# The last chunk of the down projection by seven products, a bank of its own for one product of the up projection, and another order of VectorE's and ScalarE's work between the two

## The chip, the cores and the metric

The kernel runs on one core of a Trainium2 chip. The time is that of the device for one execution, in microseconds (us); three runs of the kernel before gave 1249.63, 1249.86 and 1253.42, median 1249.86. The trace is that of one profiled execution of it.

## The reference, cut to what matters

One decoder layer on 1024 tokens of width 1024 in fp32: attention, a residual, an MLP with squared ReLU, a residual and a last RMSNorm. The change touches only what follows the attention:

```python
v = rmsnorm(h, mlp_norm_g)
hid = square(relu(v @ w_up))         # (1024 x 1024) @ (1024 x 4096)
h = h + hid @ w_down                 # (1024 x 4096) @ (4096 x 1024)
out = rmsnorm(h, final_norm_g)
```

Every fp32 operand of a matmul is held as a pair: a rounded high part and the difference to it, the low part. One product of such pairs takes three matmuls (high by high, high by low, low by high). The high part is a CAST of ScalarE (ACT), the low part a subtraction of VectorE (DVE) or GpSimd (POOL); `split2` does both.

## The kernel before

**Up.** The 4096 columns of `w_up` are done in 16 "quads" of 256 columns. A quad is a product of 2 by 2 blocks done with seven products in Winograd's form (`quads`, L1226 to L1289, one `step` for each product), each of 12 matmuls with 512 columns. Its banks in PSUM: tag "pa" (3 banks) for products 1 and 2, tag "bcd" (5 banks) for b, c and d. Product 5 goes to bank d, VectorE adds it to u2 and gets u4 (L1251); product 3 then goes on accumulating in the same bank d, and VectorE reads it once more (L1261, with u2). ScalarE copies product 1 out of "pa" (L1237, `p1`). The quads' results and their sums S1 to S4, the seven left operands of the down projection, go to DRAM (`store_hid`, `hv_dram`), queued on SyncE (SP) by `flush`. The weights of a quad are loaded and prepared one quad ahead (`weights`, `quad_w`: two loads from `w_up`, ten splits by CAST and GpSimd, four sums on VectorE, L1203 to L1206). The last two quads, 14 and 15, are done side by side, product by product; they store their four plain blocks only, to `hl_dram`, for the last chunk.

**The seam.** While quads 14 and 15 run, `w_down`'s first chunk is loaded and prepared: VectorE splits it and forms four differences of its blocks (L1373, L1376, L1379, L1382, tile `wr`), among the reads of the quads' banks. The down projection takes all eight banks of PSUM over (`dn_ps`), so its first tiles wait until VectorE has read the last bank of up.

**Down.** The 4096 rows of `w_down` are eight chunks of 512. Chunks 0 to 6 are done by `down(c)` (L1349 to L1401), with seven products in the order 1, 2, 3, 5, 7, 6, 4. A product has four tiles of 128 rows; a tile is six matmuls into a bank of its own, which VectorE adds into the accumulator of that product (`acc[i]`, L1401). For each product GpSimd makes the low part of the left operand (`ar`, L1076), VectorE or GpSimd that of the right one, and VectorE forms four differences a chunk.

**The last chunk** is done plainly, 192 matmuls (L1448 to L1455). Ahead of it the seven accumulators are folded into the four blocks of h by seven additions for each of four rows of tiles (L1423 to L1429; L1427 and L1428 on GpSimd). The first eight tiles use eight banks and go over the four parts of the contraction together; the other eight are done one by one, six or more matmuls after each other. VectorE adds each tile to its block (L1458), ScalarE squares it and sums (L1437), GpSimd makes the factor of the RMSNorm (L1439, L82, L83), VectorE multiplies (L1442, two instructions for 128 rows of the output) and SyncE stores.

Which instruction stands where on VectorE, ScalarE and GpSimd is decided by a scheduler from the program order; TensorE's order is written out by hand. Each engine then runs its own queue in order.

Of the kernel before, what the change touches and what calls it, by code (L numbers as in the profile page):

```python
# [23 lines left out]
def tile_hymba_block(  # L24
# [1316 lines left out]

    def load_acc():
# [3 lines left out]
        for q in range(4):  # L1346
            nc.gpsimd.tensor_sub(acc[4][:, q], acc[4][:, q], acc[7][:, q])

    def down(c):  # L1349
# [35 lines left out]
        for i in DORD:  # L1385
# [3 lines left out]
            prep(i)  # L1389
            for q in range(4):  # L1390
                ps = dn_ps.tile([P, 512], F32, name="dn", tag="dn")
                n = 0
                for u in range(2):
                    for a, b in ((0, 0), (0, 1), (1, 0)):
                        nc.tensor.matmul(ps[:], av[:, a, u, q * P:(q + 1) * P], bv[i][:, b, u], start=(n == 0), stop=(n == 5))  # L1395
                        n += 1
# [6 lines left out]
    for c in range(NQ // 2 - 2):  # L1403
        down(c)
    hr = [load_ar(hl_dram[:, u]) for u in range(2)]
    for u in range(2):
        split2(lh[u][:, 0], lh[u][:, 1], hr[u][:], nc.gpsimd)
    down(NQ // 2 - 2)


    lw = load_wr(NQ // 2 - 1)
    hr += [load_ar(hl_dram[:, u]) for u in range(2, 4)]
    lhr = dnr_pool.tile([P, 2, 2, T], F32R, name="lhr", tag="wr")
    lh += [lhr[:, 0], lhr[:, 1]]
    lb = []
    for u in range(4):
        lb.append(s8([P, 2, D]))
        split2(lb[u][:, 0], lb[u][:, 1], lw[:, u], nc.vector)
        if u >= 2:
            split2(lh[u][:, 0], lh[u][:, 1], hr[u][:], nc.gpsimd)  # L1420
    for q in range(4):
        g = {i: acc[i][:, q] for i in acc}
        nc.vector.tensor_add(g[2], g[2], g[1])  # L1423
        nc.vector.tensor_add(g[6], g[6], g[1])
        nc.vector.tensor_add(g[5], g[5], g[6])
        nc.vector.tensor_add(g[3], g[3], g[5])
        nc.gpsimd.tensor_add(g[4], g[4], g[6])  # L1427
        nc.gpsimd.tensor_add(g[4], g[4], g[7])  # L1428
        nc.vector.tensor_add(g[7], g[7], g[5])  # L1429
    fin = {}  # L1430

    def finish_half(t, dh, hx):
        if dh == 0:
# [4 lines left out]
        if dh == 1:
            nc.gpsimd.tensor_add(ss[:, 2:3], ss[:, 0:1], ss[:, 1:2])  # L1439
            rsqrt_mean(ss[:, 3:4], ss[:, 2:3], D, 1, nc.gpsimd)  # L1440
            for sl, hv in zip(halves, hs):
                nc.vector.scalar_tensor_tensor(y[:, sl], hv, ss[:, 3:4], gfb[:, sl], ALU.mult, ALU.mult)  # L1442
                if t == NT - 1:
                    nc.sync.dma_start(out[t * P:(t + 1) * P, sl], y[:, sl])
            if t < NT - 1:
                nc.sync.dma_start(out[t * P:(t + 1) * P, :], y[:])
# [59 lines left out]
```

## Time and profile before

| | us |
|---|---|
| median of three runs | 1249.86 |
| the profiled execution | 1253.01 |
| its span, first to last instruction | 1251.1 |
| TensorE busy | 1164.1 (93%) |
| VectorE busy | 954.6 (76%) |
| GpSimd busy | 640.7 (51%) |
| ScalarE busy | 531.6 (42%) |

Times in the rows below are microseconds from the start of the span, so 1251.1 is the end; the chunks 1 to 6 of down lie between about 950 and 1196, the last chunk from 1196.6 to 1242. "Busy" counts an engine's instructions without overlap. A wait such as "PE pd L1082 <- DVE u L1251" is idle time of TensorE ahead of the matmul of line 1082 into tile `pd`, ended by VectorE's instruction of line 1251.

### The profile page before, as it was taken

The numbers are of one execution on the slowest core, as the hardware profiler recorded it, in microseconds if no ns is written. First come the engines' busy times: TensorE is split into PE (matmuls) and PEld (weight loads), VectorE is DVE, ScalarE is ACT, GpSimd is POOL, SyncE is SP. The second block draws the span as 40 slices with busy tenths as digits, with TensorE's granted clock in tenths as the row PEclk, the third lists the DMA queues.
The fourth block names the chain that finished last, engine by engine and source line by source line (L and its number), as shares of the span: only waits on it lengthen the run. The fifth ranks groups of instructions, "written<-read, shape, count | busy, mean of one in ns | idle before, by whom it ended". The sixth has DMA issues, their size and how long they took to land. (4 is left out here: it accounts for less than half of the span.)

```text
span 1251.1 us, 15875 instructions
## 1 busy us (share of the span) xinstructions
PE 1164.1 (93%) x5448; PEld 946.6 (76%) x5448; DVE 954.6 (76%) x1302; ACT 531.6 (42%) x1078; POOL 640.7 (51%) x537
## 2 busy tenths in 40 slices
PE   9998988888799999999599999999889999999997
PEld 8887766666678888887477788777668888888875
DVE  8686499999997873564878965656386899888995
ACT  6434456666766761345422222222225333334402
POOL 3433544545643361315645654545448666668652
PEclk9999999999999999999799999999989999999999
DMA  6425734342712233674336534343658434446103
GB/s 216 130 60 183 179 80 97 77 112 48 225 46 86 68 136 135 204 249 136 130 126 206 177 122 156 123 155 129 223 193 304 153 108 167 155 166 200 53 1 135
DMA packets 100288, 176.70 MB, mean 141 GB/s; under 512 B 9072, under 2 KB 53616, under 8 KB 99440
## 3 DMA queue, kind: packets, MB, share of 16 engines
q1 hardware_dynamic: 100208, 175.70, 43.8%
q8 instruction: 43, 0.70, 0.2%
q14 instruction: 37, 0.30, 0.1%
HBM read 110.13 MB, written 52.95 MB: 130 GB/s over the span
## 5 line engine op out<-in xcount | busy, mean ns | idle before, releaser
L1395 PE MATMUL dn<-s,s 128*128 128x512 f32 x1176 | 269.9, 392 | 4.6 <-DVE ho L1278 4.3
L1395 PEld LDWEIGHTS dn<-s,s 128*128 128x128 f32 x1176 | 222.2, 189 | 52.2 <-DVE ho L1278 4.7
L1076 POOL TENSOR_TENSOR s<-s,s 128x512 fp32r<-128x512 f32 x84 | 121.4, 1462 | 113.1 <-ACT s L1075 112.9
L1076 POOL TENSOR_TENSOR s<-ar,s 128x1024 fp32r<-128x1024 f32 x49 | 131.8, 2694 | 65.2 <-ACT s L1075 65.2
L1401 DVE TENSOR_TENSOR acc<-acc,dn 128x512 f32<-128x512 f32 x184 | 117.9, 677 | 31.4 <-PE dn L1395 31.3
L1075 ACT CAST s<-s 128x512 fp32r<-128x512 f32 x84 | 49.6, 619 | 177.9 <-DMA s<-in_w_up_dram 71.0
L1075 ACT CAST s<-wr 128x1024 fp32r<-128x1024 f32 x53 | 55.6, 1052 | 146.6 <-PE dn L1395 61.0
L1082 PE MATMUL pa<-b,s 128*128 128x512 f32 x384 | 97.2, 407 | 11.8 <-ACT p L1237 4.5
L1082 PEld LDWEIGHTS pa<-b,s 128*128 128x128 f32 x384 | 74.2, 196 | 30.8 <-ACT p L1237 5.7
L542 POOL TENSOR_TENSOR b<-b,w 128x512 f32<-128x512 f32 (+2 forms) x57 | 58.0, 1018 | 60.8 <-DVE w L536 41.4
L488 PE MATMUL mm<-xh,wt 128*128 128x512 f32 x256 | 87.8, 395 | 0.0
L549 PE MATMUL tr<-zid,b 128*128 128x128 f32 x288 | 52.6, 290 | 35.1 <-DVE al L557 25.1
L549 PEld LDWEIGHTS tr<-zid,b 128*128 128x128 f32 x288 | 33.5, 143 | 57.9 <-DVE al L557 43.1
L1076 DVE TENSOR_TENSOR s<-wr,s 128x1024 fp32r<-128x1024 f32 x32 | 64.8, 2024 | 6.1 <-ACT s L1075 5.6
L1076 POOL TENSOR_TENSOR s<-wr,s 128x1024 fp32r<-128x1024 f32 x21 | 51.5, 2453 | 29.4 <-ACT s L1075 29.4
L536 DVE TENSOR_TENSOR_SCAN w<-w,zid 128x129 f32<-128x129 f32 (+1 forms) x64 | 64.7, 1014 | 1.0 <-ACT w L531 0.8
L263 PE MATMUL acc<-wt,xh 128*128 128x448 f32 (+1 forms) x256 | 62.7, 379 | 1.3 <-ACT xh L214 1.3
L1082 PE MATMUL pd<-b,s 128*128 128x512 f32 x192 | 49.5, 409 | 8.3 <-DVE u L1251 4.2
L1075 ACT CAST s<-ar 128x1024 fp32r<-128x1024 f32 x49 | 51.3, 1047 | 12.5 <-DMA ar<-hv_dram 10.7
L1082 PE MATMUL pb<-t,s 128*128 128x512 f32 x192 | 49.2, 406 | 6.8 <-ACT s L1075 6.7
L488 PEld LDWEIGHTS mm<-xh,wt 128*128 128x128 f32 x256 | 48.5, 190 | 8.3 <-issue 0.2
L263 PEld LDWEIGHTS acc<-wt,xh 128*128 128x128 f32 x256 | 47.7, 188 | 9.0 <-ACT xh L214 2.0
(349 smaller groups left out, 2800.9 us busy)
## 6 DMA issues: line engine op xcount, KB each, us to landing
ar<-hv_dram SPq DMA_DIRECT2D x49, 512.0 KB, 3.7
s<-in_w_up_dram SPq DMA_DIRECT2D x32, 512.0 KB, 4.8
wr<-in_w_down_dram SPq DMA_DIRECT2D x16, 1024.0 KB, 7.1
hv_dram<-s SPq DMA_DIRECT2D x56, 256.0 KB, 2.1
hv_dram<-ho SPq DMA_DIRECT2D x42, 256.0 KB, 2.0
wr<-in_w_in_dram SPq DMA_DIRECT2D x24, 256.0 KB, 2.9
raw<-in_w_o_dram SPq DMA_DIRECT2D x8, 512.0 KB, 3.5
ht<-h_dram SPq DMA_DIRECT2D x8, 512.0 KB, 4.2
```

The costliest lines, as they stand in the source:

```text
L263: nc.tensor.matmul(accs[t][:, :width], a[:, kk, t * P:(t + 1) * P], wts[kk][:, b, :width], start=(kk == 0 and p == 0), stop=done)
L488: nc.tensor.matmul(ps[:], wt[:, a, k % 4, :], b[:, k, tsl], start=(n == 0), stop=(n == 3 * ND - 1))
L536: nc.vector.tensor_tensor_scan(rv, rv, inject, init, ALU.mult, ALU.add)
L542: eng.tensor_mul(b[:, :n], b[:, :n], w[:, 1:n + 1])
L549: nc.tensor.transpose(tr[:, j * P:(j + 1) * P], sb_a[h, Q, C, j][:, s * P:(s + 1) * P], identf[:])
L1075: nc.scalar.copy(hi, src)
L1076: eng.tensor_sub(lo, src, f(hi))
L1082: nc.tensor.matmul(ps, w[:, a, k, :], bv[:, b, k, :], start=start and n == 0, stop=n == last, skip_group_check=True)
L1395: nc.tensor.matmul(ps[:], av[:, a, u, q * P:(q + 1) * P], bv[i][:, b, u], start=(n == 0), stop=(n == 5))
L1401: nc.vector.tensor_add(dst, dst, ps[:])
```

## The change

1. *Product 3 of up* gets a bank "e" of its own out of the same five: bank d is read once (u4), and bank e is added to u4 where bank d was added to u2.
2. *Quads 14 and 15* form and store S1 to S4 as the others do: fourteen stores where there were eight, and eight more instructions of VectorE. The second half of quad 15's weights comes after products 1 and 2 in program order. The right operands of products 5, 7, 6 and 4 of chunk 0 are prepared behind the last sum s4 of quad 15.
3. *The last chunk* is `down_last`: seven products in the order 1, 6, 5, 3, 2, 7, 4, of 24 matmuls each. Products 1, 6, 5 and 3 accumulate in the same four banks; VectorE reads each partial sum, after product 1 into acc2, after 6 into acc4, after 5 into acc7, after 3 into acc3. Product 2 has the four other banks; product 7 takes the first four, and product 4 goes on in them. The old folds are done in between, four instructions of 128 by 512 for each, queued behind the last read of their product: on GpSimd 6+=1, 4+=7, 4+=6, on VectorE 5+=6, 3+=5, 2+=1, 7+=5. The four sums of blocks of `w_down` go into a tile `lx`.
4. *The output* has four buffers where it had two; rows t = 0 are multiplied by ScalarE and GpSimd, the others by VectorE in groups of rows.

```diff
     def store_hid(q, v, ap):
         c, u = divmod(q, 2)
-        if c < NQ // 2 - 1:
-            held.append((hv_dram[c][:, v, u], ap))
-        elif v < V_S1 or v == V_A21:
-            f_, th = {V_A11: (0, 0), V_A21: (0, 1), V_A12: (1, 0), V_A22: (1, 1)}[v]
-            held.append((hl_dram[:, 2 * u + f_, th * 512:(th + 1) * 512], ap))
+        held.append((hv_dram[c][:, v, u], ap))
...
-        return w
-
-    ws_, st = {}, {}
-
-    def weights(q):
+        yield
+
+    ws_, st, wgen = {}, {}, {}
+
+    def weights(q, steps=2):
         pre = q < NPRE
-        ws_[q], st[q] = quad_w(q, pre), {}
+        if q not in ws_:
+            ws_[q], st[q] = {}, {}
+            wgen[q] = quad_w(q, pre, ws_[q])
+        for _ in range(steps):
+            next(wgen[q])
...
             elif what == 3:
-                prod(s_["d"][:], w[V_S4], B22, False, True)
+                prod(bank("e"), w[V_S4], B22, True, True)
                 s_["c12"] = o2_tile("ho")
-                nc.vector.tensor_add(s_["c12"][:], s_["d"][:], s_["u2"][:])
+                nc.vector.tensor_add(s_["c12"][:], s_["e"][:], s_["u4"][:])
                 relu2(s_["c12"][:], s_["c12"][:])
-                if q >= NQ - 2:
-                    store_hid(q, V_A21, s_["c12"][:])
-                    return
...
                 store_hid(q, V_A12, c21[:])
-                if q >= NQ - 2:
-                    return
                 s4 = o2_tile("s4")
-                nc.vector.tensor_sub(s4[:], c21[:], s_["s2"][:])
+                s_["end"] = nc.vector.tensor_sub(s4[:], c21[:], s_["s2"][:])
                 store_hid(q, V_S4, s4[:])
...
-    weights(NQ - 1)
+    weights(NQ - 1, 1)
     flush()
     last2 = [NQ - 2, NQ - 1]
     quads(last2, (1, 2))
+    weights(NQ - 1, 1)
...
     gfb = fin_pool.tile([P, D], F32, name="gfb")
-    ys = [fin_pool.tile([P, D], F32, name=f"y{n_}") for n_ in range(2)]
-    fss = [fin_pool.tile([P, 4], F32, name=f"fss{n_}") for n_ in range(2)]
+    ys = [fin_pool.tile([P, D], F32, name=f"y{n_}") for n_ in range(4)]
+    fss = [fin_pool.tile([P, 4], F32, name=f"fss{n_}") for n_ in range(4)]
     dn_pool = ctx.enter_context(tc.tile_pool(name="dn_pool", bufs=1, reuse_waits="tile"))
-    lh = [dn_pool.tile([P, 2, T], F32R, name=f"lh{u}") for u in range(2)]
...
+
+    def dn_mm(ps, av, b_, q, start):
+        n = 0
+        for u in range(2):
+            for a, b in ((0, 0), (0, 1), (1, 0)):
+                nc.tensor.matmul(ps[:], av[:, a, u, q * P:(q + 1) * P], b_[:, b, u], start=start and n == 0, stop=n == 5,
+                                 skip_group_check=True)
+                n += 1
 
     def down(c):
         if c == 0:
@@ -1386,77 +1388,105 @@
             ar = ars[i] if i in ars else load_hv(c, i)
             av = s8([P, 2, 2, 512])
             split2(av[:, 0], av[:, 1], ar[:].rearrange("p (u t) -> p u t", u=2), nc.gpsimd)
-            prep(i)
+            if c == 0 and i not in DORD[:3]:
+                with tc.issue_after(st[NQ - 1]["end"].ins):
+                    prep(i)
+            else:
+                prep(i)
...
+    def finish_half(t, dh, hx):
+        if t not in fin:
+            fin[t] = (fss[t % 4], ys[t % 4], {})
+        ss, y, hs = fin[t]
+        hs[dh] = hx
+        nc.scalar.activation(acc[6][:, t % 4], hx, AF.Square, accum_out=ss[:, dh:dh + 1])
+        if len(hs) == 2:
+            nc.gpsimd.tensor_add(ss[:, 2:3], ss[:, 0:1], ss[:, 1:2])
+            return rsqrt_mean(ss[:, 3:4], ss[:, 2:3], D, 1, nc.gpsimd)
+
+    def finish(t):
+        ss, y, hs = fin[t]
+        for d in range(2):
+            sl = halves[d]
+            if t == 0:
+                nc.scalar.activation(y[:, sl], hs[d], AF.Copy, scale=ss[:, 3:4])
+                nc.gpsimd.tensor_mul(y[:, sl], y[:, sl], gfb[:, sl])
+            else:
+                nc.vector.scalar_tensor_tensor(y[:, sl], hs[d], ss[:, 3:4], gfb[:, sl], ALU.mult, ALU.mult)
+            if t == NT - 1:
+                nc.sync.dma_start(out[t * P:(t + 1) * P, sl], y[:, sl])
+        if t < NT - 1:
+            nc.sync.dma_start(out[t * P:(t + 1) * P, :], y[:])
+
+    def down_last():
+        c = NQ // 2 - 1
+        wr = load_wr(c)
+        lx = dnr_pool.tile([P, 4, D], F32, name="lx", tag="wr")
+        w4 = wr[:].rearrange("p (u a) d -> p a u d", a=2)
+        b11, b12, b21, b22 = [w4[:, a, :, d * 512:(d + 1) * 512] for a in range(2) for d in range(2)]
+        t1, t2, t4, t3 = [lx[:, n_].rearrange("p (u d) -> p u d", u=2) for n_ in range(4)]
+        form = {1: (b11,), 6: (t2, b22, t1), 5: (t1, b12, b11), 3: (b22,), 7: (t3, b22, b12), 2: (b21,), 4: (t4, b21, t2)}
+        g = acc
+        V, G = nc.vector, nc.gpsimd
+        fold = {1: ((G, 6, 1), (G, 4, 7)), 6: ((V, 5, 6), (G, 4, 6)), 5: ((V, 3, 5),), 3: ((V, 2, 1), (V, 7, 5))}
+        for i in (1, 6, 5, 3, 2, 7, 4):
+            ar = load_hv(c, i)
+            av = s8([P, 2, 2, 512])
+            split2(av[:, 0], av[:, 1], ar[:].rearrange("p (u t) -> p u t", u=2), nc.gpsimd)
+            bv = s8([P, 2, 2, 512])
+            if i == 6:
+                nc.vector.tensor_sub(*form[5])
+            if len(form[i]) > 1 and i != 5:
+                nc.vector.tensor_sub(*form[i])
+            split2(bv[:, 0], bv[:, 1], form[i][0], nc.gpsimd if i in (3, 7, 4) else nc.vector)
+            if i in (1, 7, 2):
+                banks = [dn_ps.tile([P, 512], F32, name="dn", tag="dn") for _ in range(4)]
+                if i == 7:
+                    cbanks = banks
+            elif i == 4:
+                banks = cbanks
+            to = {1: 2, 6: 4, 5: 7, 3: 3, 7: 7, 2: 2, 4: 4}[i]
+            for q in range(4):
+                dn_mm(banks[q], av, bv, q, i in (1, 7, 2))
+                read = nc.vector.tensor_add(g[to][:, q], g[to][:, q], banks[q][:])
+                if i == 3:
+                    finish_half(q, 1, g[3][:, q])
+                elif i == 2:
+                    rs3 = finish_half(q, 0, g[2][:, q])
+                elif i == 7:
+                    finish_half(4 + q, 1, g[7][:, q])
+                elif i == 4:
+                    finish_half(4 + q, 0, g[4][:, q])
+            if i == 2:
+                with tc.issue_after(rs3.ins):
+                    finish(0)
+            elif i == 7:
+                with tc.issue_after(read.ins):
+                    for t in range(1, 4):
+                        finish(t)
+            elif i == 4:
+                with tc.issue_after(read.ins):
+                    for t in range(4, NT):
+                        finish(t)
+            with tc.issue_after(read.ins):
+                for eng, a, b in fold.get(i, ()):
+                    for q in range(4):
+                        eng.tensor_add(g[a][:, q], g[a][:, q], g[b][:, q])
...
+    down_last()
```

On VectorE, in the last chunk, before: `acc`n is the accumulator of product n, `dn` a bank of PSUM, `s8` a split operand; the folds begin while chunk 6's products 6 and 4 are still read.

```order
L1424 TENSOR_TENSOR acc6_8731<-acc6_8731,acc1_8726 128x512
L1401 TENSOR_TENSOR acc6_8731<-acc6_8731,dn_10724 128x512
L1076 TENSOR_TENSOR s8_10792<-wr_10773,s8_10792 128x1024
L1401 TENSOR_TENSOR acc4_8732<-acc4_8732,dn_10741 128x512
L1401 TENSOR_TENSOR acc4_8732<-acc4_8732,dn_10749 128x512
L1425 TENSOR_TENSOR acc5_8729<-acc5_8729,acc6_8731 128x512
L1401 TENSOR_TENSOR acc4_8732<-acc4_8732,dn_10757 128x512
L1426 TENSOR_TENSOR acc3_8728<-acc3_8728,acc5_8729 128x512
L1401 TENSOR_TENSOR acc4_8732<-acc4_8732,dn_10765 128x512
L1429 TENSOR_TENSOR acc7_8730<-acc7_8730,acc5_8729 128x512
```

And now, from the last read after product 6 to the first read after product 3:

```order
L1462 TENSOR_TENSOR acc4_8770<-acc4_8770,dn_10820 128x512
L1485 TENSOR_TENSOR acc5_8767<-acc5_8767,acc6_8769 128x512 x4
L1462 TENSOR_TENSOR acc7_8768<-acc7_8768,dn_10817 128x512
L1462 TENSOR_TENSOR acc7_8768<-acc7_8768,dn_10818 128x512
L1462 TENSOR_TENSOR acc7_8768<-acc7_8768,dn_10819 128x512
L1075 TENSOR_TENSOR s8_10996<-wr_10805,s8_10996 128x1024
L1462 TENSOR_TENSOR acc7_8768<-acc7_8768,dn_10820 128x512
L1485 TENSOR_TENSOR acc3_8766<-acc3_8766,acc5_8767 128x512 x4
L1462 TENSOR_TENSOR acc3_8766<-acc3_8766,dn_10817 128x512
```

The same banks dn_10817 to dn_10820 are read after 1, 6, 5 and 3, and four folds stand as one piece between two sets of reads of them; before, each tile had a bank that nothing continued.

On VectorE behind that, before: the last fold, the first reads of the last chunk, the first rows of the output.

```order
L1429 TENSOR_TENSOR acc7_8730<-acc7_8730,acc5_8729 128x512
L1458 TENSOR_TENSOR acc2_8727<-acc2_8727,dn_10825 128x512
L1458 TENSOR_TENSOR acc3_8728<-acc3_8728,dn_10826 128x512
L1458 TENSOR_TENSOR acc2_8727<-acc2_8727,dn_10827 128x512
L1458 TENSOR_TENSOR acc3_8728<-acc3_8728,dn_10828 128x512
L1442 SCALAR_TENSOR_TENSOR y0_8737<-acc2_8727,fss0_8739,gfb_8736 128x512
```

And now, from the last read after product 3 to the first after product 7:

```order
L1462 TENSOR_TENSOR acc3_8766<-acc3_8766,dn_10820 128x512
L1485 TENSOR_TENSOR acc2_8765<-acc2_8765,acc1_8764 128x512 x4
L1485 TENSOR_TENSOR acc7_8768<-acc7_8768,acc5_8767 128x512 x4
L1462 TENSOR_TENSOR acc2_8765<-acc2_8765,dn_10999 128x512
L1462 TENSOR_TENSOR acc2_8765<-acc2_8765,dn_11000 128x512
L1462 TENSOR_TENSOR acc2_8765<-acc2_8765,dn_11001 128x512
L1462 TENSOR_TENSOR acc2_8765<-acc2_8765,dn_11002 128x512
L1462 TENSOR_TENSOR acc7_8768<-acc7_8768,dn_11065 128x512
```

Eight folds and the reads of product 2 now stand ahead of the read of bank 11065, in which product 4 goes on.

On VectorE at the seam, before: `wr` is the chunk of `w_down`, `ho` a block of quad 14 or 15, `pd` and `pc` their banks.

```order
L1255 TENSOR_TENSOR ho_8629<-pc_8616,u4_8599 128x512
L1076 TENSOR_TENSOR s8_8807<-wr_8545,s8_8807 128x1024
L1117 SCALAR_TENSOR_TENSOR ho_8629<-ho_8629 128x512
L1255 TENSOR_TENSOR ho_8645<-pc_8632,u4_8614 128x512
L1376 TENSOR_TENSOR wr_8545<-wr_8545 128x2x512
L1117 SCALAR_TENSOR_TENSOR ho_8645<-ho_8645 128x512
L1261 TENSOR_TENSOR ho_8660<-pd_8586,u2_8569 128x512
L1117 SCALAR_TENSOR_TENSOR ho_8660<-ho_8660 128x512
L1379 TENSOR_TENSOR wr_8545<-wr_8545 128x2x512
L1261 TENSOR_TENSOR ho_8675<-pd_8601,u2_8584 128x512
L1382 TENSOR_TENSOR wr_8545<-wr_8545 128x2x512
L1117 SCALAR_TENSOR_TENSOR ho_8675<-ho_8675 128x512
```

And now, in the same place, with `pe` the new bank:

```order
L1254 TENSOR_TENSOR ho_8659<-pc_8646,u4_8628 128x512
L1112 SCALAR_TENSOR_TENSOR ho_8659<-ho_8659 128x512
L1260 TENSOR_TENSOR ho_8675<-pe_8662,u4_8613 128x512
L1112 SCALAR_TENSOR_TENSOR ho_8675<-ho_8675 128x512
L1263 TENSOR_TENSOR s1_8678<-ho_8675,ho_8643 128x512
L1266 TENSOR_TENSOR s3_8680<-ho_8520,ho_8675 128x512
L1269 TENSOR_TENSOR s2_8682<-s1_8678,ho_8520 128x512
L1260 TENSOR_TENSOR ho_8697<-pe_8684,u4_8628 128x512
L1112 SCALAR_TENSOR_TENSOR ho_8697<-ho_8697 128x512
L1263 TENSOR_TENSOR s1_8700<-ho_8697,ho_8659 128x512
L1266 TENSOR_TENSOR s3_8702<-ho_8535,ho_8697 128x512
L1269 TENSOR_TENSOR s2_8704<-s1_8700,ho_8535 128x512
```

The four differences of `wr` have gone behind the last sum of quad 15, and s1, s3 and s2 of both quads have come in.

On ScalarE where quad 15's weights are made and quad 14's bank is copied (`p1`), before:

```order
L1075 CAST s8_8452<-s8_8449 128x512 x2
L1241 ACTIVATE ho_8408<-pa_8335 128x512
L1075 CAST a22_8457<-s8_8449 128x512
L1075 CAST s8_8464<-s8_8449 128x512
L1237 COPY p1_8494<-pa_8481 128x512
L1075 CAST s8_8464<-s8_8449 128x512
```

And now:

```order
L1074 CAST s8_8466<-s8_8463 128x512 x2
L1240 ACTIVATE ho_8421<-pa_8348 128x512
L1074 CAST a22_8538<-s8_8463 128x512
L1074 CAST s8_8545<-s8_8463 128x512
L1236 COPY p1_8491<-pa_8478 128x512
L1074 CAST s8_8545<-s8_8463 128x512
```

These rows stand as they stood, but for buffer numbers.

## Rows read from the trace of the kernel before

**Rows 1.** Cores: span and mean granted clock.

```profile
core 0: 1251.1 us, clock 0.982
```

**Rows 2.** Windows: length, busy us of each engine (instructions), granted clock, DMA share, GB/s.

```profile
875.00:900.00 25.00, 20.41 (x81) 15.79 (x80) 9.10 (x11) 6.65 (x12) 12.24 (x10) 0.93 0.50 177
...
925.00:950.00 25.00, 21.94 (x86) 17.92 (x87) 13.46 (x18) 8.97 (x12) 11.49 (x6) 0.86 0.94 341
950.00:1158.00 208.00, 208.00 (x918) 171.99 (x917) 178.54 (x189) 81.15 (x84) 148.94 (x59) 1.00 0.50 166
```

**Rows 3.** PE's waits from 715 us to the end: total, times, longest.

```profile
PE pa L1082 <- ACT p L1237: 4.5, 1, 4.5
PE dn L1395 <- DVE ho L1278: 4.3, 1, 4.3
PE pd L1082 <- DVE u L1251: 4.2, 5, 1.5
...
PE dn L1453 <- DVE acc L1401: 0.7, 1, 0.7
PE dn L1395 <- DVE acc L1401: 0.4, 1, 0.4
```

**Rows 4.** SyncE in the loop of `up`: issues of the `w_up` loads.

```profile
830.90 1.51 SPq L1191 DMA_DIRECT2D s<-in_w_up_dram  x2
...
852.17 0.93 SPq L1191 DMA_DIRECT2D s<-in_w_up_dram  x2
...
872.55 0.94 SPq L1191 DMA_DIRECT2D s<-in_w_up_dram  x2
```

**Rows 5.** ScalarE around quad 14's first bank: start, duration, idle before.

```profile
884.49 0.62 ACT L1075 CAST s<-s 128x512 fp32r<-128x512 f32 x1 [4.97 <-DVE s L1203]
885.01 0.58 ACT L1237 COPY p<-pa 128x512 f32<-128x512 f32 x1
```

**Rows 6.** VectorE, the four differences of `w_down` at the seam.

```profile
909.21 3.31 DVE L1373 TENSOR_TENSOR wr<-wr 128x1024 f32<-128x1024 f32 x1
...
919.20 2.80 DVE L1376 TENSOR_TENSOR wr<-wr 128x1024 f32<-128x1024 f32 x1
...
923.85 1.22 DVE L1379 TENSOR_TENSOR wr<-wr 128x1024 f32<-128x1024 f32 x1
...
925.59 1.21 DVE L1382 TENSOR_TENSOR wr<-wr 128x1024 f32<-128x1024 f32 x1
```

**Rows 7.** Groups from 760 us on: busy, mean ns of one, idle before.

```profile
L1076 POOL TENSOR_TENSOR s<-ar,s 128x1024 fp32r<-128x1024 f32 x49 | 131.8, 2694 | 65.2 <-ACT s L1075 65.2
L1401 DVE TENSOR_TENSOR acc<-acc,dn 128x512 f32<-128x512 f32 x184 | 117.9, 677 | 31.4 <-PE dn L1395 31.3
...
L1379 DVE TENSOR_TENSOR wr<-wr 128x1024 f32<-128x1024 f32 x7 | 21.6, 3090 | 5.1 <-POOL s L1076 5.1
...
L1442 DVE SCALAR_TENSOR_TENSOR y<-acc,fss,gfb 128x512 f32<-128x512 f32 x16 | 11.3, 749 | 9.9 <-POOL fss L83 9.9
...
L1423 DVE TENSOR_TENSOR acc<-acc,acc 128x512 f32<-128x512 f32 x4 | 7.0, 1760 | 0.0
...
L1427 POOL TENSOR_TENSOR acc<-acc,acc 128x512 f32<-128x512 f32 x4 | 6.5, 1630 | 11.9 <-DVE acc L1401 7.0 <-DVE acc L1424 4.9
...
L1424 DVE TENSOR_TENSOR acc<-acc,acc 128x512 f32<-128x512 f32 x4 | 2.6, 679 | 0.0
```

**Rows 8.** VectorE's busy time in chunk 6 from one wide instruction to the last.

```profile
1148.30:1170.20 21.90, 21.61 (x20) 1.00 0.56 194
```

**Rows 9.** VectorE, a fold in chunk 6: start, duration.

```profile
1171.34 1.78 DVE L1423 TENSOR_TENSOR acc<-acc,acc 128x512 f32<-128x512 f32 x1
```

**Rows 10.** GpSimd beside it.

```profile
1170.16 2.41 POOL L1076 TENSOR_TENSOR s<-wr,s 128x1024 fp32r<-128x1024 f32 x1 [1.02 <-ACT s L1075]
```

**Rows 11.** TensorE, the last six matmuls.

```profile
1240.41 1.52 PE L1453 MATMUL dn<-s,lhr 128*128 128x512 f32 x6
```

**Rows 12.** VectorE, the last rows of the output.

```profile
1246.77 1.42 DVE L1442 SCALAR_TENSOR_TENSOR y<-acc,fss,gfb 128x512 f32<-128x512 f32 x2 [2.03 <-POOL fss L83]
```

More of the change, by code (lines that the diff above doesn't have):

```diff
@@ L82, in rsqrt_mean @@
         (eng or nc.vector).tensor_scalar(m[:, :width], ssq, 1.0 / n, EPS, ALU.mult, ALU.add)
-        nc.gpsimd.tensor_tensor(dst, m[:, :width], mhalf[:, :width], ALU.pow)
+        return nc.gpsimd.tensor_tensor(dst, m[:, :width], mhalf[:, :width], ALU.pow)
     ctx.enter_context(tc.manual_schedule(engines={mybir.EngineType.PE}))
@@ L1032, in tile_hymba_block @@
     r_dram = [dram.tile([P, HD, HT], F32, name=f"r_dram{n_}") for n_ in range(2)]
-    hv_dram = [dram.tile([P, 7, 2, 512], F32, name=f"hv_dram{c}") for c in range(NQ // 2 - 1)]
-    hl_dram = dram.tile([P, 4, T], F32, name="hl_dram")
-    V_A11, V_A12, V_A22, V_S1, V_S2, V_S3, V_S4, V_A21 = range(8)
+    hv_dram = [dram.tile([P, 7, 2, 512], F32, name=f"hv_dram{c}") for c in range(NQ // 2)]
+    V_A11, V_A12, V_A22, V_S1, V_S2, V_S3, V_S4 = range(7)
     def row_norm(pool, ht, junk, eng=None):
@@ L1186, in o2_tile, with quad_w @@
         return o2_pool.tile([P, 512], F32, name=nm, tag="o2", bufs=11)
-    def quad_w(q, pre):
+    def quad_w(q, pre, w):
         raw = s8([P, ND, 2 * P], F32)
@@ L1193, in quad_w @@
         r11, r12, r21, r22 = [raw[:, HD * d:HD * d + HD, f_ * P:f_ * P + P] for f_ in range(2) for d in range(2)]
-        w = {}
         if not pre:
@@ L1211, in quad_w @@
             w[key] = tl[:, v]
-        return w
-    ws_, st = {}, {}
-    def weights(q):
+        yield
+    ws_, st, wgen = {}, {}, {}
+    def weights(q, steps=2):
         pre = q < NPRE
-        ws_[q], st[q] = quad_w(q, pre), {}
+        if q not in ws_:
[3 more added lines that the diff above has]
+            next(wgen[q])
         if pre:
@@ L1388, in down @@
             split2(av[:, 0], av[:, 1], ar[:].rearrange("p (u t) -> p u t", u=2), nc.gpsimd)
-            prep(i)
+            if c == 0 and i not in DORD[:3]:
[3 more added lines that the diff above has]
+                prep(i)
             for q in range(4):
                 ps = dn_ps.tile([P, 512], F32, name="dn", tag="dn")
[L1392 to L1396, printed above, removed]
+                dn_mm(ps, av, bv[i], q, True)
                 dst = acc[i][:, q]
@@ L1401, in down @@
                     nc.vector.tensor_add(dst, dst, ps[:])
[L1403 to L1429, printed above, removed]
     fin = {}
     def finish_half(t, dh, hx):
-        if dh == 0:
-            fin[t] = (fss[t % 2], ys[t % 2], [])
+        if t not in fin:
+            fin[t] = (fss[t % 4], ys[t % 4], {})
@@ L1435, in finish_half @@
         ss, y, hs = fin[t]
-        hs.append(hx)
-        nc.scalar.activation(y[:, halves[dh]], hx, AF.Square, accum_out=ss[:, dh:dh + 1])
-        if dh == 1:
+        hs[dh] = hx
+        nc.scalar.activation(acc[6][:, t % 4], hx, AF.Square, accum_out=ss[:, dh:dh + 1])
+        if len(hs) == 2:
             nc.gpsimd.tensor_add(ss[:, 2:3], ss[:, 0:1], ss[:, 1:2])
[L1440 to L1446, printed above, removed]
@@ L1448, in tile_hymba_block @@
-    for group in [[(t, dh) for t in range(4) for dh in range(2)]] + [[(t, dh)] for t in range(4, NT) for dh in range(2)]:
-        banks = {k_: dn_ps.tile([P, 512], F32, name="dn", tag="dn") for k_ in group}
-        for u in range(4):
-            for t, dh in group:
-                for n, (a, b) in enumerate(((0, 0), (0, 1), (1, 0))):
-                    nc.tensor.matmul(banks[t, dh][:], lh[u][:, a, t * P:(t + 1) * P], lb[u][:, b, halves[dh]],
-                                     start=(u == 0 and n == 0), stop=(u == 3 and n == 2))
-        for t, dh in group:
-            ps = banks[t, dh]
-            hx = acc[(2, 3, 4, 7)[2 * (t // 4) + dh]][:, t % 4]
-            nc.vector.tensor_add(hx, hx, ps[:])
-            finish_half(t, dh, hx)
+            return rsqrt_mean(ss[:, 3:4], ss[:, 2:3], D, 1, nc.gpsimd)
@@ L1461 @@
+    for c in range(NQ // 2 - 1):
+        down(c)
+    down_last()
 _INS = ["x", "xT", "pos", "gcols", "gfin", "gmlp", "inv_freq", "w_in", "w_q_b", "w_kv_b", "w_o", "w_up", "w_down"]
```

## The prediction

> **What bounds the kernel now.** I read the cores first: one core, span 1251.1 us at a mean clock of 0.982, so the clock is low in a few places only [rows 1]. The windows come next. From 950 to 1158 us, in the chunks of down, TensorE is busy for all of 208.00 us with 918 matmuls: 0.2266 us each, no wait. VectorE is busy for 178.5 of the 208, GpSimd for 148.9 [rows 2]. So down is bound by TensorE, but VectorE has only 14% in hand there. Then TensorE's waits from 715 us on: 4.5 us for ScalarE's copy of product 1, 4.3 us at the seam for a bank, 4.2 us in five waits for u4, and 0.7 and 0.4 us in the last chunks for VectorE's reads [rows 3]. These are what the change can give back, beside the matmuls that it saves. Last the end: TensorE's last matmuls begin at 1240.41 and take 1.52, so they end at 1241.93, and 9.2 us pass until 1251.1 [rows 11].
>
> **Matmuls.** The last chunk goes from 192 to 7 x 24 = 168. 24 x 0.2266 = 5.4 us, on the path, since TensorE is busy there: **-5.4**. A product of 24 takes 5.44 us, a tile of six 1.36.
>
> **Stalls in the new last chunk.** Products 1, 6, 5 and 3 follow each other in the same four banks, and 4 follows 7. Each first tile waits until VectorE has read its bank, and the order shows what VectorE has queued ahead of that read. A read takes 0.64 where reads follow each other (117.9 us for 184), a fold of 512 columns 0.65 alone (2.6 for four), but 1.76 in the group that stands in chunk 6 [rows 7]. The reason is in one pair of rows: GpSimd's instruction of 1170.16 ends at 1172.57, and the fold that began at 1171.34 ends at 1173.12, 0.55 behind it [rows 9, 10]. VectorE's instructions with both inputs in SBUF take turns with GpSimd's; reads of PSUM don't (0.677 over 184 of them, whatever GpSimd does). GpSimd will be busy in the last chunk: seven low parts of `ar` at 2.69, three right operands, twelve folds at 1.63 [rows 7]. Let S be the end of chunk 6 on TensorE.
>
> - A, first tile of product 6, needs the first read after product 1. From the first read of chunk 6's product 7 (S less 16.3, plus 1.36 for the tile: S-15.0) VectorE's queue holds twelve reads and seven wide instructions, then that read. A like stretch of before, with seven wide ones and thirteen reads, took 21.9 us [rows 8]; one read less is 21.3, so the read ends at S-15.0+21.3+0.7 = S+7.0. Needed at S+5.4. Stall 1.6; 0 if the wide ones run alone, up to 9 if each takes 3.09 like the worst group [rows 7].
> - B, first tile of product 3. The last read after product 6 ends 0.7 behind that product; then four folds (F) and the read after product 5 (0.7); product 5 gives 5.44 us of cover. Stall = F + 1.4 - 5.4 = F - 4.0. Alone F is 2.6 and nothing stalls; at 1.76 it is 7.0 and 3.0 us stall; with each fold behind a GpSimd instruction of 2.4 and itself 0.6 behind that, 12 and 8. I take F = 9, since GpSimd has a split or a fold ready nearly all the time in this place: 5.0.
> - C, first tile of product 7, in the same banks, needs product 3's first read: from product 3's start three reads (1.9), a wide low part (2.2, between the 1.21 and 3.31 of [rows 6]), four folds and a read (0.7): 4.8 + F, against 10.9 of cover by products 3 and 2. With F between 7.0 and 9: 0.9 to 2.9. I take 2 (0 to 6).
> - D, first tile of product 4, needs the first read after product 7, behind three reads, eight folds and four reads. Where C has used up the slack, that is 1.9 + F8 + 2.6 + 0.7 against 5.44, so F8 - 0.2. Alone F8 is 5.2: 5.0. With one GpSimd instruction of 2.4 in the way: 7.4. Where C leaves slack, less. I take 5, the middle of the two effects (0 to 14).
>
> Sum 13.6. The 1.1 us of waits for reads that are there now [rows 3] go: **+12.5**.
>
> **A rule beside it.** The Trainium skill, page "SBUF — State Buffer", section "Who interferes with whom", says that a VectorE instruction with two inputs in SBUF contends with a GpSimd instruction that reads SBUF: whichever starts first holds the shared ports for its whole length, and the other is blocked. The rows agree (0.55 us behind GpSimd's end). By the mean of 1.76 B would be 3.0 and the sum 2 us less; by the rule with GpSimd always there first it would be 8, and the sum 3 us more. This rule speaks against four folds in one piece.
>
> **The end.** After the change, counted from product 7's first read, where product 4 starts: three reads 1.9, six multiplications of 0.71 (1.42 for two [rows 12]) 4.3, four reads 2.6, eight multiplications 5.7: 14.5. TensorE ends 5.4 behind that read, so 9.1 remain, and then the store: before, the last multiplication ends at 1246.77 + 1.42 = 1248.19, 2.9 before the end [rows 12]. 12.0 against 9.2: +2.8. If the six also take turns with GpSimd's multiplication of row 0, +2.5 more. I take **+3** (1 to 5). What would hide it is product 4 itself, if the six stood behind its reads; they stand ahead.
>
> **Up.** Product 3 in a bank of its own takes away the five waits for u4, 4.2 us by themselves [rows 3]. I count **0**. The loop runs at the pace of the weights: their loads start every 20.4 to 21.3 us [rows 4], while TensorE's seven products of 12 take 84 x 0.2266 = 19.0, and at the end of the loop the copy that ScalarE owes is itself late: it stands behind the cast that waited 4.97 us for VectorE and begins at 885.01 [rows 5]. ScalarE's order is the same there in the changed kernel. An earlier TensorE so waits longer for that copy. Bounds: -4.2, if the copy too comes earlier, and +1 for more reads in the queue.
>
> **Seam.** VectorE loses four differences there, 3.31 + 2.80 + 1.22 + 1.21 = 8.5 us [rows 6], but gets eight sums, six of them ahead of the first read that down waits for, at 0.7 alone and up to 1.76: 4.2 to 10.6. By itself -4.3 to +2 against the wait of 4.3. Also six stores more of 256 KB go into a window with the DMAs at 0.94 and 341 GB/s [rows 2]: 1.5 MB is 4.6 us there, part of it ahead of the accumulators' loads, which the first adds need. I take **-1** (-5 to +3). The four differences come again behind quad 15's last sum, where products 1, 2 and 3 of chunk 0 hide them (16 us).
>
> **Clock.** The two windows with a wait of over 4 us show a granted clock of 0.93 and 0.86 [rows 2], so mostly the level of 2.4 GHz and for a part that of 1.2, behind a wait. B and D are as long: **+1** (0 to 5).
>
> Sum: -5.4 + 12.5 + 3 + 0 - 1 + 1 = **+10.1**. The profiled execution took 1253.01, its span and 1.9; the median of the runs is 1249.86, 3.1 lower, and the difference should hold for either. Predicted: 1249.9 + 10.1 = **1260.0**. By the bounds of A to D alone (F from 2.6 to 12) the likeliest case reaches from 1253 to 1267.
>
> **Rivals.**
>
> - *The folds run alone.* If GpSimd has done its splits ahead, or its pieces fall beside reads of PSUM, F is 2.6 and A to D give nothing; the waits of 1.1 go too; the end gets +1.5, since product 4 then covers the six multiplications but not its own reads and the eight; the seam -1: -5.4 - 1.1 + 1.5 - 1 = -6.0, **1244**. For it: GpSimd has 28% in hand between 950 and 1158 [rows 2], and folds of 0.679 exist [rows 7]. Against: those 0.679 are of one line, others beside it had 1.76. It decides where four folds take up to 4.0 us. Chance 0.18. This is the other side.
> - *Up and the seam give what their waits say.* If quad 14's copy too is early, 4.2 us come back, and 4.3 at the seam instead of 1: -7.5 on top of the forecast: **1252.5**, little or no change to be seen. Against: the loads' pace and the order on ScalarE. Chance 0.09.
> - *GpSimd becomes the bound.* Ten wide pieces of 2.69 and twelve folds of 1.63 are 46.5 us in 38.1 us of matmuls. Then B is 8 and C 4.8 + 12 - 10.9 = 5.9, D 7.4, A 1.6: 22.9 - 1.1 - 5.4 + 5 - 1 + 1 = +21.4, **1271**. It is also what the rule above would give. For it: the folds of GpSimd wait for reads and then run as pieces of four, beside VectorE's own. Against: the three right operands can be made ahead. Chance 0.13.
>
> **The numbers.** The forecast holds 0.60 of the chance. A difference under 0.3%, 3.7 us, can't be told from none. Faster: the first rival and a tail of the second, 0.19. Same: most of the second that comes below the bound and the lower edge of the forecast, 0.07. Slower: the forecast, the third rival and the second's upper half, 0.74. The range for eight times in ten is 1245 to 1270: it leaves out the lower half of the first rival and the upper half of the third.
>
> **What would show it.** The profile after should show TensorE waiting for VectorE's read of line 1462 three or four times, 1.5 to 5 us each, ahead of products 6, 3, 7 and 4; folds of line 1485 with a mean over 1.4 on VectorE; the waits for u4 gone and the wait for the copy of product 1 longer (about 8 in all, as 4.5 + 4.2 now); from TensorE's end to the span's end 11 to 14 us. Wrong it is if the folds' mean stays under 1.0, if the matmuls of the last chunk run without a wait, or if the wait for the copy of product 1 doesn't grow while those for u4 go.

## The result and the profile after

Five runs of the changed kernel gave 1258.74 to 1262.48 us, median 1261.43; five of the kernel before beside them 1249.63 to 1254.89, median 1253.42. The ratio is 1.0066 with a 95% interval of 1.0041 to 1.0091: slower by 5 to 11 us by that interval, 8.0 by the medians. The profiled execution took 1262.48 us, its span is 1260.7.

TensorE's waits from 715 us to the end (total, times, longest), to be held against [rows 3]:

```profile
PE dn L1347 <- DVE acc L1462: 13.3, 3, 6.2
PE pa L1081 <- ACT p L1236: 7.7, 5, 4.5
PE dn L1347 <- DVE ho L1274: 3.4, 2, 3.0
```

The first row is new: it is the wait for VectorE's reads of the banks that are continued. The waits for u4 are gone, and the one wait of 4.5 for a copy of product 1 has become five of 7.7 in all. Where the 13.3 us lie is shown by TensorE's timeline of the last chunk (start, duration, count, idle before):

```profile
926.58 270.11 PE L1347 MATMUL dn<-s,s 128*128 128x512 f32 x1188 [0.39 <-DVE ho L1274]
1197.68 11.16 PE L1347 MATMUL dn<-s,s 128*128 128x512 f32 x48 [0.99 <-DVE acc L1462]
1215.06 19.24 PE L1347 MATMUL dn<-s,s 128*128 128x512 f32 x72 [6.22 <-DVE acc L1462]
1240.40 7.37 PE L1347 MATMUL dn<-s,s 128*128 128x512 f32 x24 [6.10 <-DVE acc L1462]
```

1164 of the first row's 1188 matmuls bring chunk 6 to its end, at 1191.1 (1196.6 before); the other 24 are product 1 of the last chunk. The waits stand ahead of product 6 (A), of product 3 (B) and of product 4 (D); there is none ahead of product 7 (C). VectorE's timeline says why:

```profile
1204.23 0.69 DVE L1462 TENSOR_TENSOR acc<-acc,dn 128x512 f32<-128x512 f32 x1 [0.56 <-POOL acc L1485]
1204.83 9.49 DVE L1485 TENSOR_TENSOR acc<-acc,acc 128x512 f32<-128x512 f32 x4
1214.24 1.87 DVE L1462 TENSOR_TENSOR acc<-acc,dn 128x512 f32<-128x512 f32 x3
...
1218.29 9.56 DVE L1485 TENSOR_TENSOR acc<-acc,acc 128x512 f32<-128x512 f32 x4
1227.77 2.47 DVE L1462 TENSOR_TENSOR acc<-acc,dn 128x512 f32<-128x512 f32 x4
1230.17 7.10 DVE L1485 TENSOR_TENSOR acc<-acc,acc 128x512 f32<-128x512 f32 x8
1237.19 4.86 DVE L1462 TENSOR_TENSOR acc<-acc,dn 128x512 f32<-128x512 f32 x8
1241.97 6.13 DVE L1426 SCALAR_TENSOR_TENSOR y<-acc,fss,gfb 128x512 f32<-128x512 f32 x6
1248.02 2.47 DVE L1462 TENSOR_TENSOR acc<-acc,dn 128x512 f32<-128x512 f32 x4
```

Four folds take 9.49 us in one piece; the first of the three reads at 1214.24 ends at 1214.9, and TensorE starts at 1215.06. The reads stand behind the folds in VectorE's queue and come behind them. The first row shows one thing more: the read after product 6 goes into acc4 and had to wait for GpSimd's fold 4+=7.

GpSimd's instructions beside the first three of these folds:

```profile
1204.15 2.41 POOL L1075 TENSOR_TENSOR s<-ar,s 128x1024 fp32r<-128x1024 f32 x1
1206.51 2.84 POOL L1075 TENSOR_TENSOR s<-wr,s 128x1024 fp32r<-128x1024 f32 x1
1209.32 2.79 POOL L1075 TENSOR_TENSOR s<-ar,s 128x1024 fp32r<-128x1024 f32 x1
```

They end at 1206.56, 1209.35 and 1212.11. The three folds, taken one by one in the same trace, begin at 1204.83, 1207.03 and 1209.83, take 2.28, 2.87 and 2.83 and so end 0.55 us behind each of these, as the pair of [rows 9, 10] did. Here VectorE gets one fold done for each instruction of GpSimd.

Windows of TensorE alone over its last pieces (length, busy us with count, granted clock, DMA share, GB/s):

```profile
1215.00:1218.00 3.00, 2.94 (x7) 0.50 0.00 0
1218.00:1221.00 3.00, 3.00 (x10) 0.67 0.00 0
1221.00:1224.00 3.00, 3.00 (x15) 1.00 0.00 0
1224.00:1234.30 10.30, 10.21 (x44) 1.00 0.01 2
1240.40:1243.00 2.60, 2.60 (x6) 0.50 0.00 0
1243.00:1247.80 4.80, 4.77 (x19) 0.91 0.00 0
```

Behind the two waits of 6 us TensorE ran at 1.2 GHz (a granted clock of 0.50), by these windows for about 5 and 3.5 us, then at 2.4 again. At full clock a matmul starts every 0.2266 us, and a piece ends some 0.16 later than that makes (six take 1.52 in [rows 11]). So 72 would be 16.5 us and took 19.24; 24 would be 5.6 and took 7.37: 4.5 us more. This also explains C. Product 3's first bank was read at 1228.4, 13.4 us behind that product's start; at full clock TensorE would have wanted it after 11.0 and waited 2.4. The slow matmuls used up that time instead.

By stages, from the starts of TensorE's rows in the two traces (us):

| | before | changed | difference |
|---|---|---|---|
| to the first product of the quads' loop | 621.77 | 625.53 | +3.8 |
| quads 0 to 5, until product 6 of quad 6 | 95.1 | 89.4 | **-5.7** |
| quads 6 to 13 | 168.8 | 169.3 | +0.6 |
| quads 14 and 15 | 36.6 | 35.7 | -0.9 |
| from down's first matmul to the end of chunk 6 | 274.4 | 271.1 | **-3.3** |
| the last chunk | 45.3 | 56.7 | **+11.4** |
| from TensorE's end (1247.77) to the end of the span | 9.2 | 12.9 | **+3.7** |
| the span | 1251.1 | 1260.7 | +9.6 |

The first row is scatter from one execution to the next: the other traces of this study, six of them of kernels that are the changed one up to there, lie between 621.0 and 623.3.

### The profile page after: what moved, and what is told of

It is laid out like the page before. It is cut to its first block, busy times and chain, and to the rows that moved or that the text cites. A ratio compares the mean times of both kernels' runs of the same rounds, so it can differ in the third digit from the quotient of the medians.

```text
span 1260.7 us, 15929 instructions
## 1 busy us (share of the span) xinstructions
PE 1163.2 (92%) x5424; PEld 947.1 (75%) x5424; DVE 983.0 (78%) x1320; ACT 537.8 (43%) x1086; POOL 669.4 (53%) x549
## 5 line engine op out<-in xcount | busy, mean ns | idle before, releaser
L1347 PE MATMUL dn<-s,s 128*128 128x512 f32 x1344 | 311.0, 394 | 16.8 <-DVE acc L1462 13.3
L1347 PEld LDWEIGHTS dn<-s,s 128*128 128x128 f32 x1344 | 254.8, 190 | 72.9 <-issue 15.8
L1075 POOL TENSOR_TENSOR s<-ar,s 128x1024 fp32r<-128x1024 f32 x56 | 149.3, 2669 | 65.8 <-ACT s L1074 51.8
L1075 DVE TENSOR_TENSOR s<-wr,s 128x1024 fp32r<-128x1024 f32 x30 | 60.9, 2029 | 4.6 <-ACT s L1074 4.6
L1266 DVE TENSOR_TENSOR s<-ho 128x512 f32<-128x512 f32 x16 | 22.8, 1427 | 53.2 <-POOL ho L1241 53.2
L1074 ACT CAST s<-ar 128x1024 fp32r<-128x1024 f32 x56 | 58.6, 1047 | 10.8 <-DMA ar<-hv_dram 8.9
```

The costliest lines, as they stand in the source:

```text
L1074: nc.scalar.copy(hi, src)
L1075: eng.tensor_sub(lo, src, f(hi))
L1266: nc.vector.tensor_sub(s3[:], s_["c11"][:], s_["c12"][:])
L1347: nc.tensor.matmul(ps[:], av[:, a, u, q * P:(q + 1) * P], b_[:, b, u], start=start and n == 0, stop=n == 5, skip_group_check=True)
```

## Experiments

Theory: VectorE's folds stand in pieces ahead of reads that TensorE needs, and are long since they take turns with GpSimd. Rivals: VectorE's work in the last chunk is too much wherever it stands; or a bank that is read and then continued costs by itself. Ratios are to the kernel before, run beside each experiment; its median there was 1253.51 or 1253.48.

**Without GpSimd's folds** (twelve folds left out):

```diff
-        fold = {1: ((G, 6, 1), (G, 4, 7)), 6: ((V, 5, 6), (G, 4, 6)), 5: ((V, 3, 5),), 3: ((V, 2, 1), (V, 7, 5))}
+        fold = {6: ((V, 5, 6),), 5: ((V, 3, 5),), 3: ((V, 2, 1), (V, 7, 5))}
```

> The changed kernel without GpSimd's twelve folds in the last chunk (6+=1, 4+=7, 4+=6 are left out, so the output is not the reference's); VectorE's sixteen folds stay where they stand. Theory (VectorE's pieces of folds stand ahead of reads that TensorE needs, and are long because they take turns with GpSimd; and the reads into acc4 wait for GpSimd's fold of acc4): the group of VectorE's folds falls from a mean of 1.70 us to about 1.0 to 1.4, the four folds after product 6 from 9.5 us to 5 to 7, TensorE's waits for the reads from 13.3 us to 3 to 6; time 1250 to 1255. Rival (VectorE's amount of work or the continued banks by themselves): the waits stay over 10 us, time 1258 or more.

Measured: 1252.95 (ratio to before 0.9993, 0.9982 to 1.0003). VectorE's same sixteen folds, in the group of the changed kernel and then of this one (busy, mean ns):

```profile
L1485 DVE TENSOR_TENSOR acc<-acc,acc 128x512 f32<-128x512 f32 x16 | 26.2, 1697 | 0.0
```

```profile
L1485 DVE TENSOR_TENSOR acc<-acc,acc 128x512 f32<-128x512 f32 x16 | 15.9, 1056 | 0.0
```

The four after product 6 take 4.69 instead of 9.49, and TensorE's waits for reads, 13.3 before this edit, are just above the range expected:

```profile
PE dn L1347 <- DVE acc L1462: 6.8, 4, 3.9
```

GpSimd's twelve folds cost VectorE 10.3 us, and TensorE half the waits. A part of that half is not the folds' length: the reads into acc4, which had waited 2.8 us for GpSimd's fold 4+=7, are free of it here.

**Without any fold** (all 28 left out):

```diff
-        fold = {1: ((G, 6, 1), (G, 4, 7)), 6: ((V, 5, 6), (G, 4, 6)), 5: ((V, 3, 5),), 3: ((V, 2, 1), (V, 7, 5))}
+        fold = {}
```

> The changed kernel without any fold in the last chunk (all 28 instructions left out, so the output is not the reference's); banks are continued as in the changed kernel. Theory: without the folds the waits for reads fall from 13.3 us to 1 to 2 (only the first tile of product 6, 1.0, stays), TensorE's last 168 matmuls run in about 39 to 40 us at full clock, time about 1261.4 - 12 - 4 = 1243 to 1247. Rival (to continue a bank that must be read in between costs by itself): 5 us or more of waits stay, time 1250 or more.

Measured: 1243.73 (0.9904 to 0.9934). One wait for a read is left, at A:

```profile
PE dn L1347 <- DVE acc L1462: 1.9, 1, 1.9
```

So continued banks cost little by themselves, and the second rival falls. The changed kernel takes 17.7 us more. In the two traces 15.4 of that lie behind chunk 6 and are the folds: 11.4 of waits, 3.2 of matmuls that are slower behind them, 0.8 at the end. The other 2 or so lie ahead of it, where the two kernels are the same.

**The folds behind the last read** (the sixteen of VectorE, and the rows of the output behind them):

```diff
-        fold = {1: ((G, 6, 1), (G, 4, 7)), 6: ((V, 5, 6), (G, 4, 6)), 5: ((V, 3, 5),), 3: ((V, 2, 1), (V, 7, 5))}
+        fold = {1: ((G, 6, 1), (G, 4, 7)), 6: ((G, 4, 6),)}
...
+        with tc.issue_after(read.ins):
+            for a, b in ((2, 1), (5, 6), (3, 5), (7, 5)):
+                for q in range(4):
+                    V.tensor_add(g[a][:, q], g[a][:, q], g[b][:, q])
...
```

> The changed kernel with VectorE's sixteen folds moved behind the last read of the last chunk, and the rows of the output behind them; GpSimd's folds stay. The same work in another place. Theory (place): TensorE's waits for reads fall from 13.3 to 1 to 4 us, as without folds, and the stretch from TensorE's last matmul to the end grows from 12.9 us by sixteen folds at 0.65 and by what the rows lose, to 25 to 30; time 1260 to 1266. Rival (amount: VectorE has too much to read and to split in the last chunk whatever the place): the waits stay over 8 us and the time goes over 1270.

Measured: 1263.67 (1.0069 to 1.0106). Its rows, of VectorE, of TensorE's last piece and of TensorE's waits for reads:

```profile
1231.17 9.71 DVE L1470 TENSOR_TENSOR acc<-acc,acc 128x512 f32<-128x512 f32 x16
```

```profile
1219.52 10.95 PE L1347 MATMUL dn<-s,s 128*128 128x512 f32 x47 [0.88 <-POOL s L1075]
```

```profile
PE dn L1347 <- DVE acc L1462: 1.0, 1, 1.0
```

TensorE ends at 1230.47, 17 us earlier, 4 of them the scatter ahead of the change; the stretch behind it grows from 12.9 to 31.6. Of this growth 9.7 us are the sixteen folds, which take 0.61 each from one to the next, with GpSimd all but idle; the rest is mostly rows of the output, of which six multiplications had run while TensorE was busy (the row of 6.13 us above). Place decides who waits, but the time is lost either way. So the first rival falls for the waits, and what it says of the time holds for the places tried.

Before, the folds hid beside the last chunk's first eight tiles, 96 matmuls, 23 us, in which TensorE needs no read of that chunk. VectorE's last fold and first reads there, and TensorE's ninth tile, the first that takes a bank again:

```profile
1216.66 0.69 DVE L1429 TENSOR_TENSOR acc<-acc,acc 128x512 f32<-128x512 f32 x1 [1.18 <-POOL acc L1428]
1217.27 2.48 DVE L1458 TENSOR_TENSOR acc<-acc,dn 128x512 f32<-128x512 f32 x4
```

```profile
1219.91 1.54 PE L1453 MATMUL dn<-s,lh 128*128 128x512 f32 x6
```

The folds end at 1217.35, and the ninth tile begins without a wait. That is the cover that seven products took away.

**Up and seam alone** (the kernel before, with these edits and its plain last chunk; quads 14 and 15 form no S1 to S4):

```diff
-                prod(s_["d"][:], w[V_S4], B22, False, True)
+                prod(bank("e"), w[V_S4], B22, True, True)
...
-                nc.vector.tensor_add(s_["c12"][:], s_["d"][:], s_["u2"][:])
+                nc.vector.tensor_add(s_["c12"][:], s_["e"][:], s_["u4"][:])
...
-                relu2(c21[:], c21[:])
+                s_["end"] = relu2(c21[:], c21[:])
...
-            prep(i)
+            if c == 0 and i not in DORD[:3]:
+                with tc.issue_after(st[NQ - 1]["end"].ins):
+                    prep(i)
+            else:
+                prep(i)
```

> The kernel before with product 3 of up in a bank of its own and with chunk 0's right operands 5, 7, 6, 4 prepared behind the last relu of quad 15, the last chunk plain as before. Theory from the trace after (chunk 6 ends 5.4 us earlier there, at 1191.2 against 1196.6): the end of chunk 6 comes 5 to 7 us earlier and the time is 1253.4 - 5 to 7 = 1246 to 1249. Rival, the -1 of the prediction: 1252 to 1253, as the waits given back are lost in other places and the eight sums of quads 14 and 15, absent here, had no part.

Measured: 1243.01 (0.9896 to 0.9926), 10.5 less than before: more than the theory gave, far more than the -1 predicted. Quads 0 to 5 take 4.4 us less in its trace, and from the first product of quad 14 to the end of chunk 6 it is 6.2 less. The wait for a bank at the seam, 4.3 before [rows 3], is

```profile
PE dn L1399 <- DVE ho L1278: 1.0, 1, 1.0
```

**The bank alone** (the first two of these edits, those of product 3):

> The kernel before with product 3 of up in a bank of its own and nothing else. Theory: up is at the pace of the weights, so the 4.2 us of waits for u4 turn into waits for the copy of product 1, quad 14 starts 0 to 1.5 us earlier than 885.64, time 1251.5 to 1253.5; the clock behind quad 14's wait doesn't rise. Rival: the waits come back as time, 4 us, 1249.5.

Measured: 1249.48 (0.9944 to 0.9974), so the rival's 4 us came true, yet not where it put them. Quads 6 to 13 take no less (169.9 us between the same matmuls; 168.8 before, 169.3 changed): there the waits for u4 did turn into waits for the copy (8.1 us in all, 4.5 before). Quads 0 to 5 take 89.7 instead of 95.1. The kernel before shows one wait of TensorE there, and what ended at that time on ScalarE and on VectorE:

```profile
648.86 4.59 PE L1082 MATMUL pd<-b,s 128*128 128x512 f32 x12 [2.43 <-ACT s L1075]
```

```profile
646.95 1.82 ACT L1075 CAST s<-s 128x512 fp32r<-128x512 f32 x3 [2.88 <-DVE s L1205]
```

```profile
648.04 0.68 DVE L1251 TENSOR_TENSOR u<-pd,u 128x512 f32<-128x512 f32 x1
```

The trace puts the wait down to a cast that ended at 648.77; the read of u4 ended at 648.72. With a bank of its own the product starts without waiting, and the same casts run on behind its start:

```profile
647.75 2.96 PE L1082 MATMUL pe<-b,s 128*128 128x512 f32 x12
```

```profile
648.38 1.82 ACT L1075 CAST s<-s 128x512 fp32r<-128x512 f32 x3 [2.89 <-DVE s L1205]
```

So the product doesn't need that cast, and it was u4 that it waited for, twice (4.0 us in these quads); behind the first wait twelve matmuls took 4.59 instead of 2.95. The waits of [rows 3] begin at 715 and leave this out. Between this run and the one ahead of it lie 6.5 us, the part of the order at the seam.

**All chunks in continued banks, no folds.** If the folds are the loss, they can be done without: read after 1, 6, 5 and 3 as in the changed last chunk, each chunk adds to the four blocks of h directly. The two sets of banks take turns, so a bank has a whole product more until it is needed. The edit is to the changed kernel; all rows of the output are multiplied by VectorE here.

```diff
+    DORD = (1, 2, 6, 7, 5, 4, 3)
+    DLAST = (1, 7, 6, 4, 5, 2, 3)
...
+    sets = [[dn_ps.tile([P, 512], F32, name=f"dn{n_}", tag="dn") for _ in range(4)] for n_ in range(2)]
+    turn = [0]
...
+            banks = sets[turn[0] % 2]
+            turn[0] += 1
+            to = {1: 2, 6: 4, 5: 7, 3: 3, 7: 7, 2: 2, 4: 4}[i]
...
```

> Every chunk is done as the last one of the changed kernel: products 1, 6, 5, 3 go on in one set of four banks and 7, 4 or 2 in the other, in turn (order 1, 2, 6, 7, 5, 4, 3; in the last chunk 1, 7, 6, 4, 5, 2, 3), so that the four accumulators hold the four blocks and no fold is left; one instruction less for each fold, none left out of the result. Theory (folds and their place are what the last chunk loses): waits for reads in the last chunk under 2 us, time as the run without folds or better, 1240 to 1245. Rival (a continued bank costs in every chunk, now that reads are late by the wide instructions in VectorE's queue): new waits of 1 us or more in each of eight chunks, time 1250 or more.

Measured: **1238.04** (0.986 to 0.9903), 15.4 less than before, the fastest kernel of this study. TensorE's waits from 875 us on:

```profile
PE pa L1081 <- ACT p L1236: 4.5, 1, 4.5
PE dn L1348 <- ACT s L1074: 1.2, 1, 1.2
PE dn L1348 <- DVE acc L1401: 1.0, 1, 1.0
PE dn L1348 <- DVE s L1075: 0.6, 1, 0.6
```

One wait for a read in eight chunks. The last chunk's 168 matmuls run without a wait in 38.2 us, where 192 took 45.3. The kernel is 5.0 us faster than up and seam alone, about the 24 matmuls less, though the two differ in more than that.

**The sums of quads 14 and 15 behind the last read** (on top of the run before; `sums` and `sum4` hold the four instructions that stood in steps 3 and 4):

```diff
...
     quads(last2, (6, 5, 7, 3, 4))
     flush()
+    with tc.issue_after(st[NQ - 1]["end"].ins):
+        for q in last2:
+            sums(q)
+            st[q]["end4"] = sum4(q)
+    flush()
...
```

> The same, with the eight sums of quads 14 and 15 behind the last read and relu of quad 15 on VectorE. Theory: the first tile of down that waits for a bank of up waits 1 us as in the run of up and seam alone, not 3.4; time 1.5 to 3 us less than with the sums ahead: 1238 to 1243. Rival: the sums, now behind, hold up the accumulators' loads or chunk 0's right operands, and as much is lost there: no difference.

Measured: 1239.26 (0.9878 to 0.9913), no difference to the run before. The theory's saving had nothing to take: with the sums ahead, the kernel has no wait at the seam at all (its four rows above); with them behind, chunk 0's operands are late: TensorE waits 2.2 us for a split of GpSimd. The rival was right.

**The first row of the output between two reads** (on top of the run before):

```diff
...
+                if last and i == 3 and q == 1:
+                    with tc.issue_after(read.ins):
+                        tail[0] = finish(0)
...
```

> The same, with the first row of the output multiplied between the second and the third read of the last product. Theory: the end behind TensorE's last matmul gets shorter by 1 to 1.5 us; time 1237 to 1242. Rival: the reads go later by the same, no difference.

Measured: 1240.14 (0.9878 to 0.9921), no difference. TensorE ends at 1226.81 and the span at 1238.3, 11.5 us; 10.4 without the edit. The row waited 1.49 us for its factor, and the reads behind it waited with it, as the rival had it.

## Why the prediction came out right, and where it was wrong

The time lies 1.4 us from the forecast of 1260.0, and that is luck in part. The forecast stood on a base of 1249.9, the median of three runs, where the five runs beside the result gave 1253.4; the change itself came out at +8.0 and not +10.1. These two errors, 3.6 and 2.1 us, nearly cancel. Inside the change two larger errors met, the last chunk and the end taken too low and up and the seam taken at next to nothing. What was right is the mechanism in the last chunk: TensorE waits for reads, the reads stand behind folds, and the folds are held by GpSimd.

- *Matmuls, -5.4*: right as far as the runs show it. The last chunk of the fastest kernel takes 38.2 us against 45.3 before; 0.7 of the difference is a wait, and about 1 is open.
- *Stalls, A 1.6, B 5, C 2, D 5*: measured 1.0, 6.2, 0, 6.1; sum 13.3 against 13.6. F was taken as 9 and measured 9.49 and 9.56 at B and C; the 2 at C are in the clock's term. The Trainium skill (page "SBUF — State Buffer", section "Who interferes with whom") would have a fold wait out a whole instruction of GpSimd each time. The trace agrees: the three folds above end 0.55 us behind the end of one. The mean fold is 2.37 even so, midway between 1.76 and the 3.0 of the prediction's worst case, since the first began when 0.7 us of GpSimd's instruction were over and the fourth took 1.74 beside a shorter one. At D eight folds took 7.10 beside one split of GpSimd, against 5.2 alone and 7.6 in the prediction's case with one instruction in the way; the wait of 6.1 lies between the 5 that it took and the 7.4 of that case.
- *The end, +3*: +3.7. The six multiplications took 6.13 beside GpSimd, not 4.3.
- *The clock, +1*: this term was too small: 4.5 us behind the waits at B and D, of which 2.4 took C's place.
- *Up, 0*: this step failed. Its reason, that TensorE would only wait longer for the copy of product 1, holds for quads 6 to 13, from which its rows came (+0.6). In quads 0 to 5 TensorE does no product 1 (it is done ahead for these), so there is no such copy to wait for, and the two waits for u4 with the slow matmuls behind the first gave 5.7 back.
- *Seam, -1*: this term too was mis-sized; -0.9 in quads 14 and 15 and -3.3 down to chunk 6's end. Without the eight sums the same stretch gave 6.2. Before, down's matmuls behind the wait of 4.3 ran in a window at 0.86 [rows 2]; with waits of 3.0 and 0.4 the same window has 1.00:

```profile
925.00:950.00 25.00, 24.61 (x109) 20.04 (x108) 17.91 (x21) 11.80 (x15) 15.91 (x8) 1.00 0.97 360
```

- *Up and seam as a rival (1252.5)*: its gain of -8.5 is near what came, -9.3 in the changed kernel by the stages (-5.7 + 0.6 - 0.9 - 3.3) and -10.5 in the kernel with these parts alone. For up that is luck: its 4.2 were the waits for u4 in quads 6 to 13, which gave nothing back, and the gain came from quads 0 to 5, ahead of [rows 3].

Last chunk and end cost +15.1, where the forecast had +11.1 (with the clock); up and seam gave 9.3, where it had 1. Together that is +5.8 in the two profiled executions, once the 3.8 of scatter ahead of the change are taken off; between the medians stand 8.0, and the 2.2 between the two are open.

## What to carry to other kernels

Matmuls saved are time only if the work that the longer matmuls covered has another place: count what each engine must do while TensorE runs without needing it, and what stands ahead of a read in the same queue. Where additions at the end are needed because results were kept apart, ask first whether the accumulator of TensorE can hold them together in every step. Read the waits over the whole stretch that an edit touches, and where two releasers end within a tenth of a microsecond, count both until a run shows which one is needed.

## What the runs showed of the hardware

An addition of VectorE of 512 columns with both inputs in SBUF takes 0.68 us where GpSimd is all but idle (mean of the sixteen folds behind the last read), 1.06 beside GpSimd's splits and 1.70 beside splits and folds; a read of PSUM stays at 0.68 in all three. Three folds that ran beside GpSimd at B each ended 0.55 us behind the end of one of its instructions. Two waits of 6 us were followed by a granted clock of 0.50 for 5 and 3.5 us, and that time can pay for a wait that would have come next, as the 2.4 us at C.
